# Wide buffers for 4 KB tiles from the MLP on, a third accumulator bank for late up-projections, and the last output block normalized on VectorE

## The chip, the cores and the metric

The kernel runs on one core of one Trainium2 chip. Its metric is the device time of one execution in microseconds (us). The core's engines are TensorE (PE, with its weight loads shown apart as PEld), VectorE (DVE), ScalarE (ACT), GpSimd (POOL) and SyncE (SP), which here only issues transfers. Each engine works through its own list of instructions in order. On-chip data lies in SBUF (128 partitions); matmul results lie in PSUM banks.

## The reference, cut to what matters

One layer of a two-branch encoder, run over two batches with the same weights: a prompt of 512 rows and a sample of 1024 rows, 1024 wide.

```python
def _trunk(x, ...):
    h = _rmsnorm(x, norm_attn_g[l])
    z = h @ w_in[l]
    ...
    a_out = _window_attn(q, k, v, bias, band, attn_sink[l])
    c = ca * jax.nn.sigmoid(cb)
    c = _dwconv(c, conv_dw_w[l], conv_dw_b[l])                # 31 taps
    c = jax.nn.silu(_layernorm(c, conv_ln_g[l], conv_ln_b[l]))
    x = x + jnp.concatenate([a_out, c], axis=-1) @ w_out[l]
    h = _rmsnorm(x, norm_ffn_g[l])
    u = _dwconv(h @ w_up[l], ffn_dw_w[l], ffn_dw_b[l])        # 3 taps
    x = x + (jax.nn.silu(u[..., :D_FF]) * u[..., D_FF:]) @ w_down[l]
    return _rmsnorm(x, norm_final_g)
```

All is float32, D_FF is 2816, and the outputs are the two normalized batches.

## The kernel before

**Precision.** A float32 product is made of three matmuls on operands split into a high and a low part (high·high, high·low, low·high). `split` does this for a weight: the raw tile comes by a transfer (`chunk_raw`, L224, 128x8x128 float32 = 512 KB), ACT makes the high part (L230, CAST), POOL subtracts it to get the low part (L231, 128x1024; for some tiles DVE does). `proj` issues the three matmuls for each of eight slices of the inner dimension (L347, L348, L350).

**Stages.** Up to about 250 us: the input projections (results in banks named b), with the convolution taps of the conv branch on DVE (L402) and ACT (L394). From about 250 to 620 us the prompt's MLP runs: 22 steps `ffn_step(k)`, each with two up-projections, a gate half and a value half (`up_half`), whose accumulators are banks u0 and u1. Of each up-projection's bank ACT makes the scaled copy with the middle tap (L973), and DVE adds the two neighbours (L969), after which the bank is free. `gate` then multiplies the halves (DVE L997, L999; POOL or DVE L1000) and stores the product in DRAM as gt0 to gt10 (L1001). Between the MLP's matmuls the attention, conv norm and out-projection of the sample are woven in as side work (`sample`): attention scores (L674, L681), the concatenated rows stored and reloaded (catd, L757, L780; ACT L766 casts them on arrival), conv norms of blocks of 128 rows (cvd loaded at L787, transposed at L804, statistics on DVE, the power of -0.5 on POOL in `rstd_of`, L214 and L215, normalized by DVE at L810, transposed back at L816), and the out-projection (L840 to L842). From about 620 to 670 us PE works off what is left of this side work.

**Pair sums.** `pair_sums(p)` loads gt of one pair (L1016, 512 KB) into a buffer of kind c, makes four sums and differences on POOL in a second buffer of kind c (L1023, L1025, L1027, L1029, each 128x256) and stores them as gb (L1030). For the pairs 0 to 6 and 10 this comes late in the prompt's stretch; pairs 7 to 9 do it at once, without the load.

**Sample's MLP and the end.** From about 680 us on the sample's MLP runs, in a fixed order on PE that is written out by hand (up-projections L1229 to L1231, down-projections L1579 to L1581), until 1483 us. At the end, for each block of 128 rows, DVE adds the last product to the running sum (L1089), and `finish` normalizes: the mean square of the right half (ACT L1637, the left half's was made before in `left_first`), the mean of both (POOL L1640), the power (POOL L1641), then ACT scales the left half (L1646) while DVE scales the right half (L1650), and SP issues both stores (L1651, 256 KB each).

**What sets the order.** `Slots` hands out named SBUF buffers: 15 of kind q (4096 bytes for each partition), 4 of kind c (4224 bytes), 61 of kind h (2048) and smaller ones. `Slots.tile` takes the smallest kind that fits and of it the one at the head of the free list. So a 4 KB tile takes a q buffer while one is free, and a c buffer only if none is. The c buffers hold the padded rows of the conv branch up to about 325 us, then the pair sums. Which instruction stands where in each engine's list is fixed when the program is built, by when its operands and its buffer come free in the build's own reckoning; SP's list too: a load that gets a buffer which has long been free moves ahead in it. From the sample's MLP on PE's order is by hand. `banks` hands out PSUM banks in the same way; `use["up"]` is the list of kinds that an up-projection may take.

Tile names as the order lists give them are buffer, number of the tile in the buffer pool, and a number of the program: `c2_620_4101` is tile 620 in buffer c2. `qsd`, `ksd`, `bbd`, `catd`, `cvd`, `x1d`, `gt`, `gb` are arrays in DRAM.

Of the kernel before, what the change touches and what calls it, by code (L numbers as in the profile page):

```python
# [15 lines left out]
P = 128  # L16
# [57 lines left out]
class Slots:  # L74
# [3 lines left out]


    def __init__(self, pool, classes, halved=None, keep=0):  # L80
        self.pool, self.free, self.n, self.clock, self.since, self.old = pool, [], 0, 0, {}, 0
        self.halved, self.keep, self.halves = halved, keep, {F32: [], F32R: []}
        for kind, (count, size) in classes.items():
            for i in range(count):
                self.free.append((f"{kind}{i}", size))
# [13 lines left out]
    def tile(self, shape, dt=F32, nbytes=4, among=None):  # L99
        self.clock += 1  # L100
        need = nbytes
        for s in shape:
            need *= s
        fits = [s for s in self.free if s[1] >= need and (among is None or s[0][0] in among)]
        least = min((s[1] for s in fits), default=0)
        slot = next((s for s in fits if s[1] == least), None)
        if self.halved and nbytes == 4 and need <= 2048:
            halves = self.halves[dt]
            wholes = [s for s in fits if s[0][0] == self.halved]
            since = self.since.get(slot[0], -OLD) if slot and slot[1] < 4096 else self.clock  # L110
            if halves and (min(h[2] for h in halves) < since or since == self.clock):
                return Half(*self.oldest(halves), shape)
            if (since == self.clock or self.clock - since < self.old) and len(wholes) > self.keep and \
                    self.since.get(wholes[0][0], -OLD) < since:
                self.split_whole(wholes[0], dt)
                return Half(*self.oldest(halves), shape)
        if slot is None:
            raise RuntimeError(f"no slot for {need} bytes")
        self.free.remove(slot)
        self.n += 1  # L120
        return Held(self, slot, (self.pool(slot[0]) if callable(self.pool) else self.pool).tile([P] + list(shape), dt, tag=slot[0], name=f"{slot[0]}_{self.n}", bufs=1))
# [52 lines left out]
def tile_hybrid_encoder(ctx: ExitStack, tc: tile.TileContext, xs, xsT, rel_bias, norm_attn_g, w_in,  # L174
# [39 lines left out]
        nc.gpsimd.tensor_scalar(out, ss, 1.0 / n, EPS, op0=ALU.mult, op1=ALU.add)  # L214
        nc.gpsimd.tensor_tensor(out, out, nhalf[:], op=ALU.pow)  # L215

    def load_x(G, tt):
        x = sb.tile([D])
        nc.sync.dma_start(x[:], G["x"][tt * P:(tt + 1) * P, :])
        return x  # L220

    def chunk_raw(src, col):
# [111 lines left out]
    def drain(queue):  # L334
        while queue:
            advance(queue)
# [604 lines left out]
    load_kv()  # L941
    drain(convs)
    sb.old = 0


    def want_up(k, half):
# [101 lines left out]
    def sample():  # L1048
        sink_columns()
        yield from attention(8, 24)  # L1050
        kt.clear(), vt.clear(), qt.clear(), bias.clear(), score_rows.clear()
        use.update(norm="a")
        pace.update(rate=RN)
        for m in range(KC + WOA):
            if m in (2, 4):
                load_cat(m // 2 + 3)
            if m < KC:
                load_wo(m, 0)
            if m >= WOA:
                split_wo(m - WOA, 0, True)  # L1060
                yield 0.0
        drain(late)
        for m in range(NE):
            yield from conv_norm(4 + m)
        load_conv(4 + NE)
        for kc in range(KC):
            load_wo(kc, 1)
            yield 0.0
# [561 lines left out]
        nc.gpsimd.tensor_scalar(rs[:, 0:1], ss[:, 0:1], 1.0 / D, EPS, op0=ALU.mult, op1=ALU.add)  # L1630
        nc.vector.tensor_tensor(part, part, fins[0][:, L], op=ALU.mult)

    def finish(blk, parts, tail):
        ss, rs, o = early.pop(blk) if tail else (sm(2), sm(2), sb.tile([D]))
        for n in range(1 if tail else 0, 2):
            s = slice(n * NT, (n + 1) * NT)
            nc.scalar.activation(o[:, s], parts[n], AF.Square, accum_out=ss[:, n:n + 1])  # L1637
        if not tail:
            nc.gpsimd.tensor_scalar(rs[:, 0:1], ss[:, 0:1], 1.0 / D, EPS, op0=ALU.mult, op1=ALU.add)
        nc.gpsimd.tensor_scalar(rs[:, 1:2], ss[:, 1:2], 1.0 / D, rs[:, 0:1], op0=ALU.mult, op1=ALU.add)  # L1640
        nc.gpsimd.tensor_tensor(rs[:, 1:2], rs[:, 1:2], nhalf[:], op=ALU.pow)  # L1641
        G, b = (GR[1], blk) if blk >= 0 else (GR[0], blk + 4)
        for n in range(2):
            s = slice(n * NT, (n + 1) * NT)
            if n == 0:
                nc.scalar.activation(o[:, s], parts[n], AF.Identity, scale=rs[:, 1:2])  # L1646
                if not tail:
                    nc.gpsimd.tensor_tensor(o[:, s], o[:, s], fins[0][:, s], op=ALU.mult)
            else:
                nc.vector.scalar_tensor_tensor(o[:, s], parts[n], rs[:, 1:2], fins[0][:, s], op0=ALU.mult, op1=ALU.mult)  # L1650
            nc.sync.dma_start(G["o"][b * P:(b + 1) * P, s], o[:, s])  # L1651
# [132 lines left out]
    for tt in (2, 3):  # L1784
        z = wide()
        for p in range(NPAIR):
            mm_down(z[:, L], 3, p, tt)
        add(cut(o12, tt), z[:, L], cut(o12, tt))
        finish(tt, (cut(o11, tt), cut(o12, tt)), True)
        del z  # L1790
    by_hand.__exit__(None, None, None)

# [53 lines left out]
```

## Time and profile before

| | us |
|---|---|
| three runs | 1492.49, 1493.83, 1494.63 (median 1493.83) |
| profiled execution, by itself | 1492.24 |
| its span (first to last instruction) | 1490.4 |
| PE busy in it | 1471.8 (99%) |
| DVE busy | 1136.2 (76%) |
| ACT busy | 798.0 (54%) |
| POOL busy | 678.0 (45%) |
| bytes moved | 225.6 MB, 151 GB/s over the span |

How to read it: the span is the time from the first to the last instruction that the profile records; 1.84 us of the profiled execution lie around it. A row of the timeline gives start, duration, engine, line of the kernel, operation, `output<-inputs` by name, shapes, a count where equal instructions follow on each other, and in brackets the idle time of the engine ahead of it with the engine and tile that ended it. A row of the waits names the waiting engine, line and bank, what it waited for, and then the sum in us, the number of times, and the longest. In the rows of windows stand the stretch, its length, the busy times of PE, PEld, DVE, ACT and POOL with instruction counts, the granted clock of PE as a share, the mean busy share of the 16 DMA engines and GB/s. `SPq` is the time that SP stands at the issue of transfers. The mean granted clock over the span is 0.998.

### The profile page before, as it was taken

What the parts mean: (1) busy time and instruction counts of PE and PEld (TensorE: products, weight loads), DVE (VectorE), ACT (ScalarE), POOL (GpSimd) and SP (SyncE); (2) the same over time, 40 slices, a digit from 0 to 9 for tenths busy, and PEclk for the clock granted to TensorE, in tenths of its full rate; (3) what the DMA queues carried; (4) which work ended last, traced back from release to release, by engine and by line L of the source; (5) the groups of instructions that cost most, each with busy time, mean ns of one, the idle gap of its engine ahead of it and who ended that gap; (6) DMA issues with size and microseconds to landing.
All of it is one profiled execution on the core that took longest, in us unless ns stands there. A gap on an engine that the chain in (4) does not pass through costs nothing.

```text
span 1490.4 us, 19857 instructions
## 1 busy us (share of the span) xinstructions
PE 1471.8 (99%) x6808; PEld 1218.8 (82%) x6808; DVE 1136.2 (76%) x1616; ACT 798.0 (54%) x1417; POOL 678.0 (45%) x540
## 2 busy tenths in 40 slices
PE   9999999999999999999999999999999999999998
PEld 7788887887888888878888888888887888888886
DVE  5999996888689975666868777777776945569884
ACT  8555656345777776444465544555445633444254
POOL 6962335235665575763326555555544000003345
PEclk9999999999999999999999999999999999999999
DMA  9953246374433347883213333333332672357644
GB/s 316 284 171 92 86 121 184 99 231 128 133 110 121 120 126 224 272 304 131 82 57 106 106 106 106 106 104 99 103 105 80 227 265 85 113 171 233 216 163 170
DMA packets 221905, 225.60 MB, mean 151 GB/s; under 512 B 12347, under 2 KB 161859, under 8 KB 221676
## 3 DMA queue, kind: packets, MB, share of 16 engines
q1 hardware_dynamic: 221804, 224.34, 47.0%
q8 instruction: 53, 0.87, 0.3%
q14 instruction: 48, 0.39, 0.1%
HBM read 165.29 MB, written 60.05 MB: 151 GB/s over the span
## 4 chain that ended last, share of the span: by engine, by line
PE 86%; DMA 5%; DVE 3%; POOL 2%; ACT 1%; issue 1%; SPq 0%; POOLq 0%; ACTq 0%; DVEq 0%
PE w L1229 9%; PE w L1231 9%; PE w L1230 9%; PE w L1580 7%; PE w L1579 7%; PE w L1581 7%; PE u L347 4%; PE u L348 4%; PE u L350 4%; PE b L347 4%; PE b L350 4%; PE b L348 4%; DMA c<-gt 2%; PE u L840 2%; PE u L842 2%; PE u L841 2%
## 5 line engine op out<-in xcount | busy, mean ns | idle before, releaser
L231 POOL TENSOR_TENSOR q<-q,q 128x1024 fp32r<-128x1024 f32 x71 | 172.9, 2439 | 122.8 <-ACT q L230 51.4
L1092 POOL TENSOR_TENSOR q<-q,q 128x512 fp32r<-128x512 f32 x101 | 141.5, 1408 | 151.2 <-ACT q L1215 140.3
L1092 DVE TENSOR_TENSOR h<-h,h 128x512 fp32r<-128x512 f32 (+2 forms) x202 | 157.4, 814 | 65.6 <-ACT h L1096 27.8
L1581 PE MATMUL w<-h,h 128*128 128x512 f32 x462 | 179.7, 389 | 0.0
L1579 PE MATMUL w<-h,h 128*128 128x512 f32 x458 | 178.2, 389 | 0.0
L1580 PE MATMUL w<-h,h 128*128 128x512 f32 x458 | 178.2, 389 | 0.0
L1229 PE MATMUL w<-h,q 128*128 128x512 f32 x448 | 174.9, 390 | 1.3 <-ACT w L1312 1.1
L1231 PE MATMUL w<-h,q 128*128 128x512 f32 x448 | 174.3, 389 | 0.0
L1230 PE MATMUL w<-h,q 128*128 128x512 f32 x426 | 165.8, 389 | 0.0
L402 DVE SCALAR_TENSOR_TENSOR c<-c,cvw,c 128x512 f32<-128x512 f32 x209 | 157.0, 751 | 3.1
L347 PE MATMUL u<-h,q 128*128 128x512 f32 x368 | 146.9, 399 | 1.9 <-DVE h L969 1.9
L348 PE MATMUL u<-h,q 128*128 128x512 f32 x368 | 144.0, 391 | 0.0
L350 PE MATMUL u<-h,q 128*128 128x512 f32 x360 | 141.2, 392 | 0.0
L1089 POOL TENSOR_TENSOR q<-q,q 128x1024 f32<-128x1024 f32 x12 | 33.1, 2772 | 229.4 <-DVE q L1089 212.9
L1096 ACT CAST h<-h 128x512 fp32r<-128x512 f32 x120 | 72.1, 622 | 97.1 <-DVE h L1092 40.5
L347 PE MATMUL b<-h,q 128*128 128x512 f32 x264 | 104.9, 397 | 0.9 <-DVE q L437 0.9
L230 ACT CAST q<-q 128x1024 fp32r<-128x1024 f32 (+1 forms) x73 | 75.7, 1041 | 54.5 <-POOL q L231 20.6
L348 PE MATMUL b<-h,q 128*128 128x512 f32 x264 | 103.7, 393 | 0.0
L350 PE MATMUL b<-h,q 128*128 128x512 f32 x264 | 103.5, 393 | 0.0
L1581 PEld LDWEIGHTS w<-h,h 128*128 128x128 f32 x462 | 86.7, 188 | 18.0
L1579 PEld LDWEIGHTS w<-h,h 128*128 128x128 f32 x458 | 86.0, 188 | 18.0
L1580 PEld LDWEIGHTS w<-h,h 128*128 128x128 f32 x458 | 86.0, 188 | 17.7
(443 smaller groups left out, 3625.1 us busy)
## 6 DMA issues: line engine op xcount, KB each, us to landing
q<-in_w_up SPq DMA_DIRECT2D x88, 512.0 KB, 4.3
ga<-q SPq DMA_DIRECT2D x64, 256.0 KB, 2.0
h<-ga SPq DMA_DIRECT2D x57, 256.0 KB, 3.4
q<-in_w_in SPq DMA_DIRECT2D x28, 512.0 KB, 5.1
h<-in_w_down SPq DMA_DIRECT2D x52, 256.0 KB, 4.0
q<-in_x_sample SPq DMA_DIRECT2D x15, 512.0 KB, 6.2
h<-qsd SPq DMA_DIRECT2D x23, 256.0 KB, 3.3
x1d<-q SPq DMA_DIRECT2D x11, 512.0 KB, 5.2
```

What stands on the lines that cost most here:

```text
L231: ins = (nc.vector if dve else nc.gpsimd).tensor_tensor(lo[:], raw[:], hi[:].bitcast(F32), op=ALU.subtract)
L347: nc.tensor.matmul(out, whi[:, kc, :], hi[:], start=(kc == 0), stop=False)
L348: nc.tensor.matmul(out, whi[:, kc, :], lo[:], start=False, stop=False)
L350: nc.tensor.matmul(out, wlo[:, kc, :], hi[:], start=False, stop=(kc == KC - 1))
L402: nc.vector.scalar_tensor_tensor(acc[:], src(t), w(t), acc[:], op0=ALU.mult, op1=ALU.add)
L1092: (eng or nc.vector).tensor_tensor(out, a, b, op=ALU.subtract)
L1229: nc.tensor.matmul(out, whi[:, s], hi[:], start=(start and c == 0), stop=False, **go)
L1230: nc.tensor.matmul(out, whi[:, s], lo[:], start=False, stop=False, **go)
L1231: nc.tensor.matmul(out, wlo[:, s], hi[:], start=False, stop=(stop and c == 3), **go)
L1579: nc.tensor.matmul(out, sh[:, c], th[:], start=(p == 0), stop=False)
L1580: nc.tensor.matmul(out, sh[:, c], tl[:], start=False, stop=False)
L1581: nc.tensor.matmul(out, sl[:, c], th[:], start=False, stop=(p == NPAIR - 1))
```

## The change

It has three parts. First, `Slots` gets a field `wide`, 0 until the prompt's MLP begins and 1 from there on: a tile that would take a 4 KB buffer may then take a c buffer instead, if more than one of those is free and the c buffer has been free for longer. Second, in `sample`, after `drain(late)` (about 590 us), `use.update(up="uc")` lets up-projections take the bank c0 besides u0 and u1. Third, `finish` gets `pieces`, true for the sample's fourth block alone, the last to be finished: the mean square of its right half, added to the left half's, comes from one VectorE instruction, so that POOL has only the power to do; DVE makes the right half in two quarters of 128x256, each stored at once by SP, and ACT issues the store of the left half. (`load_x` also gets an argument `halves`, which no caller sets.)

```diff
@@ -78,7 +78,7 @@
 
 
     def __init__(self, pool, classes, halved=None, keep=0):
-        self.pool, self.free, self.n, self.clock, self.since, self.old = pool, [], 0, 0, {}, 0
+        self.pool, self.free, self.n, self.clock, self.since, self.old, self.wide = pool, [], 0, 0, {}, 0, 0
         self.halved, self.keep, self.halves = halved, keep, {F32: [], F32R: []}
         for kind, (count, size) in classes.items():
             for i in range(count):
@@ -104,6 +104,10 @@
         fits = [s for s in self.free if s[1] >= need and (among is None or s[0][0] in among)]
         least = min((s[1] for s in fits), default=0)
         slot = next((s for s in fits if s[1] == least), None)
+        if slot and least == 4096 and among is None and self.wide:
+            spare = [s for s in fits if s[1] > least]
+            if len(spare) > self.wide:
+                slot = min([slot] + spare, key=lambda s: self.since.get(s[0], -OLD))
         if self.halved and nbytes == 4 and need <= 2048:
             halves = self.halves[dt]
             wholes = [s for s in fits if s[0][0] == self.halved]
@@ -214,9 +218,16 @@
         nc.gpsimd.tensor_scalar(out, ss, 1.0 / n, EPS, op0=ALU.mult, op1=ALU.add)
         nc.gpsimd.tensor_tensor(out, out, nhalf[:], op=ALU.pow)
 
-    def load_x(G, tt):
+    def power(out):
+        nc.gpsimd.tensor_tensor(out, out, nhalf[:], op=ALU.pow)
+
+    def mean_square(x, junk, so_far, out):
+        nc.vector.tensor_tensor_reduce(junk, x, x, 1.0 / D, so_far, ALU.mult, ALU.add, out)
+
+    def load_x(G, tt, halves=False):
         x = sb.tile([D])
-        nc.sync.dma_start(x[:], G["x"][tt * P:(tt + 1) * P, :])
+        for s in (slice(0, NT), slice(NT, D)) if halves else (slice(0, D),):
+            nc.sync.dma_start(x[:, s], G["x"][tt * P:(tt + 1) * P, s])
         return x
 
     def chunk_raw(src, col):
@@ -941,6 +952,7 @@
     load_kv()
     drain(convs)
     sb.old = 0
+    sb.wide = 1
 
 
     def want_up(k, half):
@@ -1060,6 +1072,7 @@
                 split_wo(m - WOA, 0, True)
                 yield 0.0
         drain(late)
+        use.update(up="uc")
         for m in range(NE):
             yield from conv_norm(4 + m)
         load_conv(4 + NE)
@@ -1630,15 +1643,18 @@
         nc.gpsimd.tensor_scalar(rs[:, 0:1], ss[:, 0:1], 1.0 / D, EPS, op0=ALU.mult, op1=ALU.add)
         nc.vector.tensor_tensor(part, part, fins[0][:, L], op=ALU.mult)
 
-    def finish(blk, parts, tail):
+    def finish(blk, parts, tail, pieces=False):
         ss, rs, o = early.pop(blk) if tail else (sm(2), sm(2), sb.tile([D]))
-        for n in range(1 if tail else 0, 2):
-            s = slice(n * NT, (n + 1) * NT)
-            nc.scalar.activation(o[:, s], parts[n], AF.Square, accum_out=ss[:, n:n + 1])
-        if not tail:
-            nc.gpsimd.tensor_scalar(rs[:, 0:1], ss[:, 0:1], 1.0 / D, EPS, op0=ALU.mult, op1=ALU.add)
-        nc.gpsimd.tensor_scalar(rs[:, 1:2], ss[:, 1:2], 1.0 / D, rs[:, 0:1], op0=ALU.mult, op1=ALU.add)
-        nc.gpsimd.tensor_tensor(rs[:, 1:2], rs[:, 1:2], nhalf[:], op=ALU.pow)
+        if pieces:
+            mean_square(parts[1], o[:, R], rs[:, 0:1], rs[:, 1:2])
+        else:
+            for n in range(1 if tail else 0, 2):
+                s = slice(n * NT, (n + 1) * NT)
+                nc.scalar.activation(o[:, s], parts[n], AF.Square, accum_out=ss[:, n:n + 1])
+            if not tail:
+                nc.gpsimd.tensor_scalar(rs[:, 0:1], ss[:, 0:1], 1.0 / D, EPS, op0=ALU.mult, op1=ALU.add)
+            nc.gpsimd.tensor_scalar(rs[:, 1:2], ss[:, 1:2], 1.0 / D, rs[:, 0:1], op0=ALU.mult, op1=ALU.add)
+        power(rs[:, 1:2])
         G, b = (GR[1], blk) if blk >= 0 else (GR[0], blk + 4)
         for n in range(2):
             s = slice(n * NT, (n + 1) * NT)
@@ -1646,6 +1662,15 @@
                 nc.scalar.activation(o[:, s], parts[n], AF.Identity, scale=rs[:, 1:2])
                 if not tail:
                     nc.gpsimd.tensor_tensor(o[:, s], o[:, s], fins[0][:, s], op=ALU.mult)
+                if pieces:
+                    nc.scalar.dma_start(G["o"][b * P:(b + 1) * P, s], o[:, s])
+                    continue
+            elif pieces:
+                for h in (slice(NT, NT + HT), slice(NT + HT, W2)):
+                    nc.vector.scalar_tensor_tensor(o[:, h], parts[n][:, h.start - NT:h.stop - NT], rs[:, 1:2],
+                                                   fins[0][:, h], op0=ALU.mult, op1=ALU.mult)
+                    nc.sync.dma_start(G["o"][b * P:(b + 1) * P, h], o[:, h])
+                continue
             else:
                 nc.vector.scalar_tensor_tensor(o[:, s], parts[n], rs[:, 1:2], fins[0][:, s], op0=ALU.mult, op1=ALU.mult)
             nc.sync.dma_start(G["o"][b * P:(b + 1) * P, s], o[:, s])
@@ -1786,7 +1811,7 @@
         for p in range(NPAIR):
             mm_down(z[:, L], 3, p, tt)
         add(cut(o12, tt), z[:, L], cut(o12, tt))
-        finish(tt, (cut(o11, tt), cut(o12, tt)), True)
+        finish(tt, (cut(o11, tt), cut(o12, tt)), True, tt == 3)
         del z
     by_hand.__exit__(None, None, None)
 
```

The lists of instructions hold the same work but for the last block: PE has as many instructions as before, DVE three more, POOL one fewer. Of 2166 tiles 396 get another buffer, the first of them the raw tile 594 of w_up. PE's list differs only by rows that change places locally, from about 255 us on. The engines' lists change as follows at the places below. Line numbers of the changed kernel are larger by 11 to 13 from `chunk_raw` up to `finish` (L224 is L235, L347 is L358, L1016 is L1028, L1029 is L1041); L214 and L215 are L218 and L219.

SP's list at about 328 us: loads of queries and keys for the sample's attention (qsd, ksd, into q and h buffers) and three raw tiles of w_up. Before:

```order
L638 DMA h38_549_3651<-qsd1_164 128x512
L623 DMA h17_517_3434<-bbd_400 128x384
L638 DMA h51_578_3841<-qsd1_164 128x512
L877 DMA q9_501_3377<-ksd_167 64x1024 x2
L638 DMA h59_556_3698<-qsd1_164 128x512
L224 DMA q13_525_3510<-in_w_up 128x8x128
L224 DMA q4_510_3420<-in_w_up 128x8x128
L224 DMA q7_519_3438<-in_w_up 128x8x128
```

and now:

```order
L649 DMA h38_549_3651<-qsd1_164 128x512
L634 DMA h17_517_3434<-bbd_400 128x384
L235 DMA c2_620_4101<-in_w_up 128x8x128
L649 DMA h51_578_3841<-qsd1_164 128x512
L888 DMA q9_501_3377<-ksd_167 64x1024 x2
L649 DMA h59_556_3698<-qsd1_164 128x512
L235 DMA q13_525_3510<-in_w_up 128x8x128
L235 DMA q4_510_3420<-in_w_up 128x8x128
L235 DMA q7_519_3438<-in_w_up 128x8x128
```

The raw tile 620 of w_up, before taken into buffer q14 18 rows further on, stands in c2 ahead of three loads of the attention and of the three raw tiles 525, 510 and 519.

PE's list at about 617 us, where the up-projections 346, 348 and 350 are the prompt's last, a1_352 is a transpose of a conv norm, and c0_358 is an out-projection. Before:

```order
L350 MATMUL u0_346_6305<-h10_494_3319,q7_952_6221 128x512
L804 MATMUL a1_352_6473<-ident_91,h56_1007_6461 128x128 x4
L840 MATMUL c0_358_6612<-h22_963_6259,h1_994_6387 128x512
L841 MATMUL c0_358_6612<-h25_964_6260,h1_994_6387 128x512
L842 MATMUL c0_358_6612<-h22_963_6259,h18_995_6388 128x512
L840 MATMUL c0_358_6612<-h24_966_6271,h1_994_6387 128x512
L347 MATMUL u1_348_6370<-h5_478_3229,q6_974_6301 128x512
```

and now:

```order
L361 MATMUL u0_346_6305<-h10_494_3319,c3_952_6221 128x512
L361 MATMUL c0_350_6425<-h5_478_3229,q4_987_6353 128x512
L358 MATMUL c0_350_6425<-h12_480_3238,q8_986_6352 128x512
L359 MATMUL c0_350_6425<-h20_481_3239,q8_986_6352 128x512
L361 MATMUL c0_350_6425<-h12_480_3238,q4_987_6353 128x512
L358 MATMUL c0_350_6425<-h9_484_3259,q8_986_6352 128x512
L359 MATMUL c0_350_6425<-h8_485_3260,q8_986_6352 128x512
L358 MATMUL u1_348_6370<-h5_478_3229,q14_974_6301 128x512
```

The up-projection 350, before in u0 behind the other two, now has its own bank c0 and six of its matmuls stand between the end of 346 and the start of 348; the out-projection c0_358 comes later.

SP's list where the load of pair 1's gt stands (tile 1066): before behind the store gb8, at about 606 us, into buffer c2:

```order
L1030 DMA gb8_3409<-c2_937_6113 128x1024
L1016 DMA c2_1066_6760<-gt1_3391 128x1024
L224 DMA q10_954_6230<-in_w_up 128x8x128
L787 DMA h36_1020_6541<-cvd1_170 128x4x128
L780 DMA h34_1021_6543<-catd_168 128x512
```

and now behind the load of the x_sample block 1124, which in before's list was issued at about 633 us, into buffer c0, which held the sums stored as gb9:

```order
L1042 DMA gb9_3410<-c0_989_6362 128x1024
L876 DMA h37_1025_6568<-in_w_out 64x512 x2
L878 DMA h31_1030_6598<-in_w_out 128x512
L878 DMA h26_1031_6600<-in_w_out 128x512
L230 DMA q8_1124_7075<-in_x_sample 128x1024
L1028 DMA c0_1066_6760<-gt1_3391 128x1024
L1042 DMA gb2_3403<-c3_1102_6957 128x1024
```

That load has moved down by more than 20 rows of SP's list. POOL's list at about 650 us, with the last sums of pair 3 (tile 1120), the sums of pair 6 (tile 1169) and the power for a conv norm (s10_1060). Before:

```order
L1025 TENSOR_TENSOR c3_1120_7066<-c2_1117_7045 128x256
L1027 TENSOR_TENSOR c3_1120_7066<-c3_1120_7066,c2_1117_7045 128x256
L1029 TENSOR_TENSOR c3_1120_7066<-c2_1117_7045,c3_1120_7066 128x256
L1000 TENSOR_TENSOR h45_1029_6593<-h45_1029_6593,h57_1028_6588 128x512
L1023 TENSOR_TENSOR c0_1169_7346<-c1_1168_7344 128x256
L1025 TENSOR_TENSOR c0_1169_7346<-c1_1168_7344 128x256
L1027 TENSOR_TENSOR c0_1169_7346<-c0_1169_7346,c1_1168_7344 128x256
L214 TENSOR_SCALAR s10_1060_6692<-s8_1059_6691 128x1
L1029 TENSOR_TENSOR c0_1169_7346<-c1_1168_7344,c0_1169_7346 128x256
L215 TENSOR_TENSOR s10_1060_6692<-s10_1060_6692,nhalf_92 128x1
```

and now:

```order
L1035 TENSOR_TENSOR c2_1120_7066<-c0_1117_7045 128x256
L1037 TENSOR_TENSOR c2_1120_7066<-c0_1117_7045 128x256
L1039 TENSOR_TENSOR c2_1120_7066<-c2_1120_7066,c0_1117_7045 128x256
L1041 TENSOR_TENSOR c2_1120_7066<-c0_1117_7045,c2_1120_7066 128x256
L218 TENSOR_SCALAR s10_1060_6692<-s8_1059_6691 128x1
L219 TENSOR_TENSOR s10_1060_6692<-s10_1060_6692,nhalf_92 128x1
L1035 TENSOR_TENSOR c3_1169_7346<-c1_1168_7344 128x256
L1037 TENSOR_TENSOR c3_1169_7346<-c1_1168_7344 128x256
L1039 TENSOR_TENSOR c3_1169_7346<-c3_1169_7346,c1_1168_7344 128x256
L1041 TENSOR_TENSOR c3_1169_7346<-c1_1168_7344,c3_1169_7346 128x256
```

Both rows of the power now stand ahead of the sums of pair 6, and behind those of pair 3; before, they stood among those of pair 6. Elsewhere: the raw tile 594 is loaded about at 250 us, ahead of loads of w_out; between the store of gb7 and the load of catd rows into tile 957 (567 to 578 us) SP issued four loads of 512 KB, the tiles 913, 1064 (gt0), 985 and 917, and issues five now, 917, 1053, 990, 1036 and 933, of which 1036 and 1053 are x_sample blocks that came between 614 and 620 us; and DVE's L810 for the conv norm at about 677 us (with POOL's power for it) stands one place ahead of a scaling of rows (L1110).

## The prediction

> **What bounds the kernel now.** The page comes first: PE is busy for nearly the whole span.
>
> ```profile
> span 1490.4 us, 19857 instructions
> PE 1471.8 (99%) x6808; PEld 1218.8 (82%) x6808; DVE 1136.2 (76%) x1616; ACT 798.0 (54%) x1417; POOL 678.0 (45%) x540
> ```
>
> All that PE doesn't do is 18.6 us, and start and end hold most of it. The change touches the stretch from 240 us on, so I read PE's waits from there to PE's end, and the windows of that stretch.
>
> ```profile
> PE u L347 <- DVE h L969: 1.9, 3, 0.7
> PE a L816 <- DVE h L810: 1.0, 2, 0.5
> PE u L840 <- ACT h L230: 0.4, 1, 0.4
> ...
> 240.00:730.00 490.00, 486.06 (x2312) 403.22 (x2311) 375.29 (x633) 287.30 (x536) 270.62 (x210) 1.00 0.52 164
> 326.00:342.00 16.00, 15.48 (x82) 12.79 (x81) 10.07 (x14) 8.66 (x12) 12.34 (x9) 1.00 1.06 335
> 567.00:570.50 3.50, 3.50 (x19) 2.96 (x18) 2.00 (x6) 2.47 (x6) 1.69 (x1) 1.00 0.55 196
> 570.50:584.50 14.00, 14.00 (x72) 11.70 (x71) 6.33 (x14) 8.07 (x17) 8.77 (x7) 1.00 1.00 283
> 612.00:660.00 48.00, 46.63 (x215) 37.47 (x213) 29.92 (x43) 16.33 (x31) 35.62 (x41) 1.00 0.94 316
> ```
>
> The reader is to see two things. Buffers and banks can take from PE only those few waits, 3.3 us by these three rows. And the DMA engines, half idle on the whole (0.52), are full at three places (1.06, 1.00, 0.94): there a load put ahead delays those behind it. The granted clock is 1.00 throughout, so it is no term.
>
> **The sum is made against the profiled execution**, 1492.24 us, of which 1.84 lie outside the span; the median of the runs, 1493.83, is 1.59 above it. I add the terms to the median. A difference under 0.2% (3.0 us: from 1490.8 to 1496.8) can't be told from none.
>
> **Part A, the last block.** Nothing covers it: PE is done.
>
> ```profile
> 1483.47 0.69 DVE L1089 TENSOR_TENSOR q<-w,q 128x512 f32<-128x512 f32 x1 [1.82 <-PE w L1581]
> 1485.37 0.55 POOL L1641 TENSOR_TENSOR s<-s,nhalf 128x1 f32<-128x1 f32 x1
> 1485.95 0.75 DVE L1650 SCALAR_TENSOR_TENSOR q<-q,s,c 128x512 f32<-128x512 f32 x1 [1.79 <-POOL s L1641]
> 1486.70 0.81 SPq L1651 DMA_DIRECT2D out_sample<-q  x2
> ...
> L681 DVE CUSTOM_DVE_ANT_0 q<-a,h,nsink 128x384 f32<-128x384 f32 x31 | 18.7, 615 | 4.5 <-PE a L674 4.3
> L681 DVE CUSTOM_DVE_ANT_0 q<-a,h,nsink 128x256 f32<-128x256 f32 x13 | 6.0, 481 | 2.9 <-PE a L674 2.9
> L681 DVE DVE_READ_ACCUMULATOR2_ANT s<- 128x1 f32 x96 | 8.1, 84 | 0.0
> L1092 DVE TENSOR_TENSOR h<-h,h 128x256 fp32r<-128x256 f32 x7 | 2.9, 420 | 3.4 <-ACT h L1563 1.8 <-PE w L1580 1.6
> ```
>
> The trace has no such reduction. Its nearest rows are the attention's reducing instruction: 481 ns at 256 columns, 615 at 384, so 134 for 128 more and an estimated 0.75 us at 512, and 0.08 for reading the accumulator. The add ends at 1484.16; 0.83 of reduction and an estimated 0.13 to reach POOL (POOL's own handover to DVE took 0.03, from 1485.92 to 1485.95) put the power's start at 1485.13, against 1485.37 in the row: 0.24 earlier. Then come the scalings. Before, both halves ended near 1486.70 and SP needed 0.81 for both stores, to 1487.51. Now the first quarter (0.42, by the 128x256 row) ends near 1486.13, the second near 1486.55, SP issues them by 1486.95 (0.40 each), and ACT issues the left half beside it. So the last issue ends 0.56 earlier. I take −0.5. The upper bound comes from the landing:
>
> ```profile
> out_sample<-q SPq DMA_DIRECT2D x8, 256.0 KB, 2.2
> x1d<-q SPq DMA_DIRECT2D x11, 512.0 KB, 5.2
> ```
>
> A store that ACT issues isn't in the trace. The nearest row is the same store issued by SP, 2.2; the far one is 5.2, 3.0 more: ACT's issue ends 0.66 before 1487.51, so the end would be 2.3 later (the bound below is −0.6). I go by 2.2, since bytes and target are the same. [...]
>
> **Part B, the load of tile 594 at 250 us.**
>
> ```profile
> 257.68 0.50 PE L840 MATMUL u<-h,h 128*128 128x512 f32 x1 [0.39 <-ACT h L230]
> ```
>
> A w_out load is what this wait hangs on, through ACT's cast. 512 KB more ahead of it cost 0.52 MB at 335 GB/s, 1.56 us. But PE's list now has nine more matmuls ahead of this one, and at 490 us for 2312 they cover 1.9 us. I take 0. Bounds: −0.4 (the wait goes and the load finds idle DMA) and +1.5 (no cover).
>
> **Part C, the load of tile 620 at 328 us.** Here the DMA engines are full.
>
> ```profile
> 332.20 4.64 SPq L224 DMA_DIRECT2D q<-in_w_up  x3
> 339.91 1.05 ACT L230 CAST q<-q 128x1024 fp32r<-128x1024 f32 x1 [4.89 <-DMA q<-in_w_up]
> 345.39 0.47 PE L347 MATMUL u<-h,q 128*128 128x512 f32 x1 [0.61 <-DVE h L969]
> 352.20 0.47 PE L347 MATMUL u<-h,q 128*128 128x512 f32 x1 [0.62 <-DVE h L969]
> ```
>
> ACT's list stands still for 4.89 us for such a load, L973 for the up-projection is queued behind its casts, DVE's L969 behind that, and PE waits for L969. All three are in order, so 1.56 us more of DMA reach PE whole: +1.56. The second wait (352.20) goes, because on DVE one conv tap (L402) moves from between the two L969 to ahead of the first, where DVE idles anyway: −0.62. Together +0.94. Bounds: −1.23 (the load costs nothing and both waits go) and +1.56. [...]
>
> **Part D, five loads for four between 567 and 578 us.**
>
> ```profile
> 578.30 0.58 SPq L780 DMA_DIRECT2D h<-catd  x1
> 583.88 0.62 ACT L766 CAST h<-h 128x512 fp32r<-128x512 f32 x1 [4.47 <-DMA h<-catd]
> 587.68 0.75 DVE L969 SCALAR_TENSOR_TENSOR h<-u,fw,h 128x511 f32<-128x511 f32 x1
> 589.90 0.48 PE L347 MATMUL u<-h,q 128*128 128x512 f32 x1
> ```
>
> ACT waits for the catd rows, and the next L973 and L969 stand behind. 0.52 MB more at 283 GB/s are 1.85 us; the first loads now fall into 567 to 570.5 at share 0.55, where 0.45 × 3.5 = 1.6 us are free: 0.25 late. L969 ends at 588.43 and PE needs it at 589.90, a margin of 1.47. So 0; without the idle stretch it is 0.4.
>
> **Part E, the third bank.**
>
> ```profile
> 617.29 0.48 PE L347 MATMUL u<-h,q 128*128 128x512 f32 x1 [0.69 <-DVE h L969]
> ```
>
> PE waits here for u1 to come free. Six matmuls of 350 now stand ahead, 1.3 us of work that needs no such bank; the waiting is 0.69 and goes. −0.69, or 0 if the split of tile 987 for it is late.
>
> **Part F, POOL between 628 and 680 us.**
>
> ```profile
> 631.75 0.74 POOL L1023 TENSOR_TENSOR c<-c 128x256 f32<-128x256 f32 x1 [0.49 <-DMA gb<-c]
> 634.42 1.29 POOL L1029 TENSOR_TENSOR c<-c,c 128x256 f32<-128x256 f32 x1
> 654.13 0.55 POOL L215 TENSOR_TENSOR s<-s,nhalf 128x1 f32<-128x1 f32 x1
> 654.72 0.81 DVE L810 TENSOR_SCALAR h<-a,s,s 128x512 f32<-128x512 f32 x1 [2.83 <-POOL s L215]
> 655.67 0.63 PE L816 MATMUL a<-ident,h 128*128 128x128 f32 x4 [0.54 <-DVE h L810]
> ...
> 632.73 0.60 SPq L219 DMA_DIRECT2D q<-in_x_sample  x1
> ...
> c<-gt SPq DMA_DIRECT2D x8, 512.0 KB, 6.9
> ```
>
> The power now runs ahead of pair 6's sums: by itself that ends the wait of 0.54 at 655.67. But pair 1's gt is loaded only behind an x_sample load, at 633.3 by this row. Landing after 6.9 (the median) at 640.2, its four sums, 3.96 us from 631.75 to 635.71, end at 644.2 instead; gt3 takes the same buffer (0.4, then 6.9, then 3.96) and ends at 655.4, and the power behind it at about 656.3 instead of 654.68: +1.6. On the other hand two x_sample blocks have left the stretch (share 0.94). With landings one us shorter the power ends at 654.3. I take 0 for this wait and −0.4 for the second one of the row L816, 1.0 − 0.54, where the power of a conv norm moves ahead of others. F is −0.4, bounds −0.95 and +1.6.
>
> **The rest.** In the steady steps the w_up loads come earlier and PE doesn't wait; 0. In the sample's MLP the changed buffers stand ahead of no wait on them: 0.
>
> **Sum:** −0.5 + 0 + 0.94 + 0 − 0.69 − 0.4 = −0.65, or 1491.6 for the profiled execution and **1493.2** by the median.
>
> **The rivals.**
>
> *Faster: an early load is free.* The DMA share is 0.52, so those behind catch up. A −0.5, B −0.4, C −1.23, E −0.69, F −0.95: −3.8, 1490.0. For it: over the whole stretch half the DMA is free. Against it: ACT's 4.89 us in a window at 1.06. Chance 0.20. [...]
>
> *Slower: the pair sums hold POOL.* The wide buffers that now go to split weights are missing for gt1, and POOL in order stands before the sums of pair 1 and of pair 3, with the powers for the conv norms behind. In before one gt took longer than the median:
>
> ```profile
> 649.24 3.01 SPq L1016 DMA_DIRECT2D c<-gt  x1
> 658.12 0.74 POOL L1023 TENSOR_TENSOR c<-c 128x256 f32<-128x256 f32 x1 [3.44 <-DMA c<-gt]
> ```
>
> That is 8.9 us from issue to use. Two links of 8.9 end the power at 633.3 + 8.9 + 3.96 + 0.4 + 8.9 + 3.96 + 0.9 = 660.3, 5.6 later; with A, C and E the sum is +5.35, 1499.2. It decides once the power ends later than 657.9 (F above +3.2). For it: the median alone gives 656.3. Against: less is in flight. 0.12.
>
> *ACT's store lands late:* A is +2.3 instead of −0.5, 1496.0. 0.08.
>
> *It does nothing:* buffers and banks aren't what PE waits for and the tail's reduction is no shorter: 1493.8. 0.05.
>
> **How the numbers follow.** The forecast keeps 0.55. Its own bounds reach from 1490.6 (all lower ends) to about 1497 (ends above combined as roots of squares: 2.8, 1.5, 0.6, 0.4, 0.7 and 2.0 give 3.8). The range takes in the faster rival and ACT's late store and leaves out the slower one: 1489.8 to 1497.0. Faster is the first rival, 0.20; slower the second, 0.12; the same is the rest, 0.68.
>
> **What would show it.** Right: no PE wait on L981 (which was L969) near 352 and 617, one of about 2.2 near 345; the last issue ended 0.5 sooner after the last matmul; the power for the transpose near 655 between 653.5 and 655.5 when moved to before's clock. Wrong: pair 3's sums ending past 657, an ACT store landing over 3 us after its issue, or waits at places that had none, above all for a split at the prompt's last up-projections.

## The result: slower by 0.8%, and the profile after

The changed kernel took 1504.18 us (median of six runs, 1501.48 to 1506.29), the kernel before 1492.59 beside it (six runs, 1491.95 to 1494.63). The ratio is 1.0078, 95% interval 1.0068 to 1.0089. The profiled execution of the changed kernel has a span of 1503.0 us against 1490.4. The page and the waits of PE from 230 us on, in the same form as before:

```profile
span 1503.0 us, 19863 instructions
...
PE u L358 <- DVE h L981: 3.5, 1, 3.5
PE u L358 <- DVE s L818: 3.1, 1, 3.1
PE w L1242 <- ACT w L1325: 2.2, 1, 2.2
PE t L1165 <- DVE h L1105: 1.3, 1, 1.3
PE u L361 <- POOL c L242: 1.0, 1, 1.0
PE w L1242 <- ACT h L1334: 0.9, 1, 0.9
```

Few waits, but long ones: 13.0 us in all (1.0 of it in small rows left out here), against 5.4 before. That is 7.6 of the 12.6 us by which the span grew. The rest shows only in the windows behind the three longest waits. The first number behind the last pair of brackets is the granted clock:

```profile
346.00:350.00 4.00, 2.97 (x7) 2.42 (x8) 3.90 (x9) 2.24 (x3) 4.00 (x3) 0.51 0.21 63
350.00:354.00 4.00, 4.00 (x13) 3.11 (x13) 3.67 (x7) 1.65 (x3) 2.92 (x2) 0.63 0.01 2
354.00:358.00 4.00, 4.00 (x21) 3.37 (x20) 2.66 (x10) 2.31 (x7) 0.45 (x1) 1.00 0.22 49
...
626.00:630.00 4.00, 4.00 (x12) 3.12 (x11) 3.85 (x6) 0.74 (x2) 3.70 (x6) 0.57 0.82 295
630.00:634.00 4.00, 4.00 (x21) 3.31 (x20) 0.72 (x2) 1.16 (x3) 2.20 (x3) 1.00 0.86 293
...
812.00:818.00 6.00, 4.38 (x12) 3.48 (x13) 5.93 (x6) 2.11 (x4) 3.03 (x2) 0.72 0.44 171
```

PE counts as busy in them and does little: 13 matmuls in the 4 us from 350 on and 12 from 626 on, where at 0.227 us for each some 18 of 512 columns fit. Added up matmul by matmul, the extra time behind the three waits is 2.85, 1.75 and 1.7 us, 6.3 us in all. Waits and lower clock, 13.9, less 0.4 gained at the end and 0.8 at the start give 12.7 of the 12.6 us. (PE stood at 257.5 instead of 258.7 us by its 1225th matmul; 0.4 of these 1.2 is a wait that is counted already. This start isn't the change's: 0.5 of it is there at 108 us, before the change acts, and the rest also shows in two later runs that have before's order up to 1200 us.)

**The place at 345 us.** SP, ACT and PE in the changed kernel:

```profile
328.16 0.44 SPq L235 DMA_DIRECT2D c<-in_w_up  x1
341.58 1.05 ACT L241 CAST q<-q 128x1024 fp32r<-128x1024 f32 x1 [7.79 <-DMA q<-in_w_up]
347.03 0.77 PE L358 MATMUL u<-h,q 128*128 128x512 f32 x1 [3.49 <-DVE h L981]
```

The first row is the load of tile 620 that moved ahead. ACT's cast comes at 341.58 instead of 339.91, 1.67 us later, and PE waits until 347.03 instead of 345.39. One pair of profiles doesn't show how much of this is the load: further down, the same wait differs by 1.4 us between executions with one order.

**The place at 615 us.** POOL, DVE, SP and PE, and the landing of the gb stores between 596 and 640 us:

```profile
606.69 0.33 SPq L1042 DMA_DIRECT2D gb<-c  x1
...
DMA to landing us min/median/max: 2.7/5.3/6.5
...
613.33 2.37 POOL L242 TENSOR_TENSOR c<-q,q 128x1024 fp32r<-128x1024 f32 x1 [6.66 <-DVE h L981]
615.75 0.50 PE L361 MATMUL u<-h,c 128*128 128x512 f32 x1 [1.04 <-POOL c L242]
616.90 5.20 POOL L242 TENSOR_TENSOR q<-q,q 128x1024 fp32r<-128x1024 f32 x2
616.98 5.67 DVE L242 TENSOR_TENSOR h<-h,h 128x512 fp32r<-128x512 f32 x2 [3.09 <-POOL h L1012]
625.50 0.47 PE L358 MATMUL u<-h,q 128*128 128x512 f32 x1 [3.10 <-DVE s L818]
```

POOL stands still for 6.66 us ahead of the subtraction that writes the low part 952 into c3. The row names DVE, but what this instruction waits for by the program are the raw tile and the store of gb8 out of c3. The store, issued at 606.69 and the slowest of the four (6.5), lands at 613.2; POOL's wait for the semaphore of that landing ends at 613.24, and POOL starts at 613.33. Then PE waits 1.04 for the subtraction. POOL then makes its two other subtractions back to back, and two of DVE's, which take 0.68 each alone, last 5.67 together beside them. The taps that free u1 stand behind them on DVE: 3.10 us.

**The place at 811 us**, in the sample's MLP:

```profile
803.34 2.88 POOL L1105 TENSOR_TENSOR q<-q,q 128x512 fp32r<-128x512 f32 x2 [2.57 <-ACT q L1228]
804.99 0.38 SPq L1192 DMA_DIRECT2D q<-in_w_up  x1
808.90 0.69 DVE L1105 TENSOR_TENSOR h<-q 128x512 f32<-128x512 f32 x1 [5.09 <-DMA q<-in_w_up]
813.00 0.57 ACT L1325 COPY w<-w 128x512 f32<-128x512 f32 x1 [5.32 <-DVE q L1372]
813.62 0.71 PE L1242 MATMUL w<-h,q 128*128 128x512 f32 x1 [2.24 <-ACT w L1325]
```

A split of raw tile 6 runs late on ACT and POOL, to 804.96; the load of raw tile 12 takes the same buffer and is issued at 804.99; DVE waits 5.09 for it with the taps L1371 and L1372 queued behind, ACT for these, PE for ACT. Before, the longest wait of PE in this MLP was

```profile
PE w L1229 <- ACT w L1312: 1.1, 1, 1.1
```

**The end**, where the last block is finished:

```profile
1497.19 0.75 DVE L225 CUSTOM_DVE_ANT_0 q<-q,s 128x512 f32<-128x512 f32 x1
1498.03 0.55 POOL L222 TENSOR_TENSOR s<-s,nhalf 128x1 f32<-128x1 f32 x1 [6.60 <-DVE s L225]
1499.13 0.81 SPq L1672 DMA_DIRECT2D out_sample<-q  x2
1499.36 0.37 ACTq L1666 DMA_DIRECT2D out_sample<-q  x1
...
out_sample<-q ACTq DMA_DIRECT2D x1, 256.0 KB, 2.2
```

From PE's end (1496.42) to the span's end it is 6.57 us, against 7.00 before.

### The profile page after: what moved, and what is told of

Same layout as the page of the kernel before. It is cut to its first block, busy times and chain, and to the rows that moved or that the text cites. A ratio compares the mean times of both kernels' runs of the same rounds, so it can differ in the third digit from the quotient of the medians.

```text
span 1503.0 us, 19863 instructions
## 1 busy us (share of the span) xinstructions
PE 1478.0 (98%) x6808; PEld 1223.3 (81%) x6808; DVE 1130.6 (75%) x1619; ACT 794.5 (53%) x1415; POOL 679.4 (45%) x539
## 4 chain that ended last, share of the span: by engine, by line
PE 88%; DVE 4%; issue 2%; DMA 2%; POOL 2%; ACT 1%; SPq 0%; POOLq 0%; DVEq 0%; ACTq 0%
PE w L1242 8%; PE w L1243 8%; PE w L1244 8%; PE w L1594 7%; PE w L1592 7%; PE w L1593 7%; PE u L358 5%; PE u L359 5%; PE u L361 5%; PE b L358 4%; PE b L361 4%; PE b L359 4%; PE u L853 2%; PE u L851 2%; PE u L852 2%
## 5 line engine op out<-in xcount | busy, mean ns | idle before, releaser
L242 POOL TENSOR_TENSOR q<-q,q 128x1024 fp32r<-128x1024 f32 x51 | 124.0, 2438 | 98.6 <-ACT q L241 65.3
L1105 POOL TENSOR_TENSOR q<-q,q 128x512 fp32r<-128x512 f32 x72 | 100.4, 1397 | 123.1 <-ACT q L1228 120.4
L361 PE MATMUL u<-h,q 128*128 128x512 f32 x336 | 132.7, 395 | 0.0
L358 PE MATMUL u<-h,q 128*128 128x512 f32 x312 | 125.9, 404 | 6.6 <-DVE h L981 3.5
L1242 PE MATMUL w<-h,q 128*128 128x512 f32 x308 | 121.2, 394 | 3.3 <-ACT w L1325 2.2
L359 PE MATMUL u<-h,q 128*128 128x512 f32 x312 | 123.9, 397 | 0.0
L1244 PE MATMUL w<-h,q 128*128 128x512 f32 x308 | 120.4, 391 | 0.0
L1243 PE MATMUL w<-h,q 128*128 128x512 f32 x299 | 117.1, 392 | 0.0
L1105 POOL TENSOR_TENSOR c<-q,c 128x512 fp32r<-128x512 f32 x56 | 79.6, 1422 | 73.0 <-ACT c L1228 72.0
L358 PE MATMUL b<-h,q 128*128 128x512 f32 x264 | 104.8, 397 | 0.9 <-DVE q L448 0.9
L1102 POOL TENSOR_TENSOR q<-c,q 128x1024 f32<-128x1024 f32 x2 | 4.8, 2392 | 210.6 <-DVE c L1102 210.6
```

Source lines behind the costliest of these rows:

```text
L242: ins = (nc.vector if dve else nc.gpsimd).tensor_tensor(lo[:], raw[:], hi[:].bitcast(F32), op=ALU.subtract)
L358: nc.tensor.matmul(out, whi[:, kc, :], hi[:], start=(kc == 0), stop=False)
L359: nc.tensor.matmul(out, whi[:, kc, :], lo[:], start=False, stop=False)
L361: nc.tensor.matmul(out, wlo[:, kc, :], hi[:], start=False, stop=(kc == KC - 1))
L1105: (eng or nc.vector).tensor_tensor(out, a, b, op=ALU.subtract)
L1242: nc.tensor.matmul(out, whi[:, s], hi[:], start=(start and c == 0), stop=False, **go)
```

## The experiments

**Theory A:** the wide buffers cost all of it, in two ways: they put transfers and instructions behind work that they didn't wait for before, and PE's waits that come of it are followed by a lower clock. **Rival B:** the third bank and the finish do. **Rival C:** the loads' order is of no matter.

### Without the wide buffers

```diff
-    sb.wide = 1
```

> The change without its first part: wide stays 0, the third bank and the new finish are kept. Theory A (the wide buffers cost all of it, by waits and by the clock that falls behind the long ones): 1491.5 to 1493, no lower clock after 340, 620 and 810 us. Rival B (the third bank lets PE run into the wait of 3.1 us at 622 us of the changed kernel, and the tail does the rest): about 1497 to 1498, with the wait of PE on u1 still over 2 us there. The tail (PE's end to the span's end) 6.6 us by both, as in the changed kernel, against 7.0.

1492.07 us, ratio 0.9999 (0.9990 to 1.0008). PE's longest wait from 230 us on is 1.17 and the clock isn't lowered behind any:

```profile
PE u L358 <- DVE h L980: 2.6, 3, 1.2
PE a L827 <- DVE h L821: 0.9, 2, 0.6
...
618.78 0.47 PE L358 MATMUL u<-h,q 128*128 128x512 f32 x1 [1.17 <-DVE h L980]
```

So all of the slowdown needs the wide buffers; B falls. The third bank by itself doesn't take the wait at 617 us away: it is 1.17 here, 0.69 before.

### The wide buffers alone

```diff
-        use.update(up="uc")
...
-        finish(tt, (cut(o11, tt), cut(o12, tt)), True, tt == 3)
+        finish(tt, (cut(o11, tt), cut(o12, tt)), True)
```

> The first part alone: wide buffers, no third bank, the old finish. A: 1503 to 1506, with the waits of PE near 343, 614 to 625 and 811 us. B: about 1497 to 1499, the wait at 622 us gone or under 1 us.

1506.47 us, ratio 1.0094 (1.0080 to 1.0108): 0.5 us above A's range and far from B's, with waits of 4.3, 1.1, 3.1 and 2.3 us at the same places. The wait on u1 is there without the third bank.

### The low part 952 not in a wide buffer

```diff
-        if slot and least == 4096 and among is None and self.wide:
+        if slot and least == 4096 and among is None and self.wide and self.n + 1 not in (952,):
```

> The whole change, but the low part 952 of one weight may not take a wide buffer. A, with the chain store gb8 to buffer c3 to POOL's subtraction to DVE to PE at 614 to 626 us as one of three places: POOL's idle time of 6.7 us there goes, PE's waits of 1.0 and 3.1 us go, the clock stays at 1.00 there, and the kernel is 3.5 to 5.5 us faster than the changed one, about 1499. B: the wait on u1 stays, since six matmuls of the third bank's projection cover only 1.3 us; no more than 1 us faster, about 1503.

1503.11 us, ratio 1.0070 (1.0055 to 1.0086): by time at most about 1 us better than the changed kernel (the two intervals overlap), as B expected and not the 3.5 to 5.5 of A; by the trace the chain is gone as A expected. No wait on u1 is left and the clock at 626 is 1.00. But two others took its place: 1.6 us at 619, for the cast of the weight of projection 350, whose load was issued at 611.7, and this one:

```profile
658.69 0.55 POOL L219 TENSOR_TENSOR s<-s,nhalf 128x1 f32<-128x1 f32 x1
660.23 0.63 PE L827 MATMUL a<-ident,h 128*128 128x128 f32 x4 [2.27 <-DVE h L821]
...
626.00:630.00 4.00, 4.00 (x21) 3.37 (x20) 2.98 (x5) 2.50 (x6) 2.74 (x4) 1.00 0.84 268
660.00:664.00 4.00, 3.52 (x12) 2.65 (x13) 2.76 (x6) 2.65 (x6) 0.35 (x2) 0.70 0.83 277
```

This is the prediction's slower rival: the conv norm's power on POOL behind pair sums that are late. In the changed kernel PE was itself too late by then to see it.

### The raw tile 620 not in a wide buffer

The same line with `(620,)`.

> The whole change, but the raw tile 620 may not take a wide buffer, so that its load goes back behind the three loads that ACT waits for at about 340 us. A: PE's wait of 3.5 us at 343 us falls to about 1.5 (the 0.6 of before and what PE has gained ahead of it), the clock stays at 1.00 there, the kernel is 3 to 4 us faster than the changed one, about 1500.5. Rival C (the DMA is full there whatever its order, and ACT's list waits as long): the wait stays over 2.5 us and the time at 1504.

1502.92 us, ratio 1.0075 (1.0061 to 1.0088). The wait at 343 us is 2.07 us in the profiled execution, with no lower clock behind it, and its span is 1500.4, 2.6 shorter. The runs don't confirm that: by time this is inconclusive. 2.07 instead of 3.49 speaks against C, but one profile doesn't settle it, as the next run shows.

### One load alone

The kernel before with one tile forced into c2:

```diff
+        if slot and least == 4096 and among is None and self.wide and self.n + 1 == 620:
+            spare = [s for s in fits if s[0] in ("c2", "c3")]
+            if spare:
+                slot = min(spare)
```

> The kernel before, with one thing of the change: the raw tile 620 is loaded into buffer c2, ahead of the three loads that ACT waits for at about 340 us; no third bank, the old finish. By the sum of the prediction the load of 512 KB costs 1.56 us in the DMA queues and the wait at 345 us becomes 2.2 us instead of 0.6. Clock theory (a wait of PE of about 2.05 us or more is followed by some 3 us of matmuls at nearly half the rate): this lies on the edge, +1.6 us without and +3.3 with the fall, 1493.8 to 1495.5. Rival (an early load is free): no change, 1492.2, wait 0.6.

1494.37 us against 1491.39, ratio 1.0018 (1.0007 to 1.0029), about 2.7 us:

```profile
345.07 0.47 PE L358 MATMUL u<-h,q 128*128 128x512 f32 x1 [1.94 <-DVE h L981]
345.00:349.00 4.00, 3.93 (x11) 3.16 (x12) 3.87 (x9) 2.77 (x5) 4.00 (x3) 0.61 0.32 96
```

The wait of 0.6 is one of 1.94, and 11 matmuls stand in the 4 us behind it. But the load isn't all that differs: SP's and PE's lists change at further places too. And the profiled execution is the fastest of its ten (1490.57): by its matmuls PE loses 2.1 us at 345 and has them back by 700 us. That the 2.7 us of the runs arise at this place isn't shown.

The wait also varies with nothing changed. Here it is in the two runs with set waits (below), which have before's order up to 1200 us; the second is followed by a lower clock:

```profile
345.25 0.47 PE L347 MATMUL u<-h,q 128*128 128x512 f32 x1 [1.60 <-DVE h L969]
346.98 0.47 PE L347 MATMUL u<-h,q 128*128 128x512 f32 x1 [2.02 <-DVE h L969]
```

So all twelve profiles have to be taken together. In the six with a load of w_up moved ahead at this place the wait is 1.94 to 4.30 us, 3.15 on the mean; in the six without, 0.61 to 2.38, 1.58 on the mean. By these an early load costs about 1.6 us here and isn't free.

### Wide only up to the sample's MLP

```diff
     h2.pop((0, 0))
+    sb.wide = 0
```

> The whole change, but wide goes back to 0 when the sample's MLP begins. A with the fourth place put down to choices made in that MLP: PE's wait of 2.2 us at 811 us and the lower clock after it go, about 1500. A with that place put down to the buffers that the prompt's part leaves behind: the wait stays, 1504.

1497.34 us, ratio 1.0039 (1.0028 to 1.0050), faster than either expectation. PE's waits of 1.3, 2.2 and 0.9 us after 690 us are gone; the longest that is left there is

```profile
PE w L1243 <- ACT w L1326: 0.8, 1, 0.8
```

About half of the slowdown came of buffers handed out in the sample's MLP, in which the prediction had put 0.

### The three places mended

All of it: neither 620 nor 952 wide, and wide off at the sample's MLP.

> The whole change, but the tiles 620 and 952 may not take a wide buffer and wide goes back to 0 at the sample's MLP. A: the waits over 2.05 us near 343 and 622 us go and with them the lower clock there; what is left is the power at about 657 us (2.3 us of wait when 952 alone is narrow) and, if the fourth place stays, 811 us. 1496 to 1499. If all long waits went: about 1492.5, the same as before.

1495.27 us, ratio 1.0023 (1.0013 to 1.0034), 0.7 below A's range. Waits of 2.4 us at 345, 2.3 at 619 and 2.7 at 662 are left, with a lower clock behind the first two. A had the long waits at the first two places go, and missed: with both tiles narrow PE still waits there.

### Wide in the middle of the prompt only

```diff
-    sb.wide = 1
...
     for k in range(NJ):
+        sb.wide = int(4 <= k < 18)
...
+    sb.wide = 0
```

> The whole change, but wide is 1 only during the prompt's steps 4 to 17 of 22. The load of tile 624 now takes buffer c2, free since 325 us, and stands in SP's list where 620 stood, though its step comes 25 us later. Theory (what counts is since when the buffer is free, not when the rule is switched on): PE waits 2.4 to 3.5 us near 345, mostly with a lower clock after it, no other wait over 1.5 us from there on, 1494.5 to 1496.5. Rival (switched on after the place, the rule does no harm and the early loads of the steady steps even help): 0.6 us of wait at 345, 1490 to 1492.

1495.28 us against 1490.55, ratio 1.0028 (1.0015 to 1.0041). PE waits 3.3 us at 346, with 1.7 us lost behind it, and 1.9 at 640, which wasn't expected. The load of tile 624 stands where 620 stood. So it isn't the moment at which the rule is switched on that counts, but since when the buffer is free; and no gain from the early loads of the steady steps shows.

### Waits of a set length

The kernel before, with a chain of VectorE operations that add zero to an operand of the down-projections, one in each of six products:

```diff
...
+            if w == 0:
+                th = hl[i, NPAIR - 2][1][0]
+                for n in STALL[i]:
+                    nc.vector.scalar_tensor_tensor(th[:, 0:n], z[:, W2 - n:W2], 0.0, th[:, 0:n].bitcast(F32), op0=ALU.mult, op1=ALU.add)
...
```

> The kernel before, with six chains of VectorE put ahead of an operand of the down-projections, so that PE waits once in each of six products, for about 1.2, 1.9, 2.3, 2.6, 3.3 and 4.7 us (products 2, 5, 6, 7, 4 and 1); nothing is left out. Clock theory: the waits up to about 1.9 us cost just themselves and the clock stays at 1.00; those from 2.3 us on are followed by matmuls 0.43 us apart instead of 0.23 for 3 to 5 us, 1.5 to 2.9 us more each, in all about 16 us of waits and 7 to 10 us of lower clock. Rival (the lower clock of the changed kernel has nothing to do with its waits): the clock stays at 1.00 after all six, or falls where there was none.

> As the run with six long waits, but with chains of 128, 256, 384, 640, 896 and 1536 columns (products 2, 5, 6, 7, 4 and 1); nothing is left out. By the waits seen so far (below 1.8 us none of eight was followed by a lower clock, from 1.8 to 2.6 some were, from 2.7 on nearly all): waits of about 1.2 to 3.1 us, none of those below 1.8 followed by a lower clock, one or two of those between 1.8 and 2.6. Rival (a sharp threshold): all above one length, none below it.

Two waits of the first of these runs with the window behind each:

```profile
1315.19 0.50 PE L1579 MATMUL w<-h,h 128*128 128x512 f32 x1 [2.53 <-DVE h L1684]
1410.72 0.80 PE L1579 MATMUL w<-h,h 128*128 128x512 f32 x1 [3.21 <-DVE h L1684]
1315.00:1319.00 4.00, 3.81 (x17) 3.17 (x18) 0.82 (x2) 2.40 (x3) 0.00 (x0) 1.00 0.00 0
1410.50:1414.50 4.00, 3.78 (x9) 3.00 (x10) 1.30 (x2) 0.62 (x1) 2.38 (x1) 0.50 0.00 0
```

Two of the second, with windows of 3.41 us each, the one in which most of the wait lies and the next:

```profile
1398.30 0.50 PE L1579 MATMUL w<-h,h 128*128 128x512 f32 x1 [2.01 <-DVE h L1684]
1447.22 0.50 PE L1579 MATMUL w<-h,h 128*128 128x512 f32 x1 [2.12 <-DVE h L1684]
1395.40:1398.81 3.41, 1.40 (x6) 0.85 (x6) 2.74 (x5) 0.62 (x1) 0.00 (x0) 1.00 0.15 56
1398.81:1402.22 3.41, 3.41 (x9) 2.68 (x9) 0.57 (x1) 0.62 (x1) 2.37 (x1) 0.50 0.06 17
1443.19:1446.60 3.41, 1.91 (x9) 1.25 (x7) 3.21 (x6) 1.72 (x4) 0.00 (x0) 1.00 0.93 281
1446.60:1450.01 3.41, 2.79 (x12) 2.29 (x13) 2.92 (x3) 0.17 (x1) 0.00 (x0) 1.00 0.51 191
```

Waits made on purpose lower the clock: after 1.83, 3.21, 3.43 and 6.60 us in the first run (1.7, 2.9, 2.8 and 3.0 us lost), after 2.23 and 2.01 in the second (1.7 each). After 1.97 and 2.53 in the first, and 0.65, 0.97, 1.46 and 2.12 in the second, it stays at 1.00. So the cause is the wait, but not its length alone. The lengths didn't come out as meant: 1.83 to 6.60 us in the first run for 1.2 to 4.7, 0.65 to 2.23 in the second for 1.2 to 3.1.

What the two kinds differ in is shown by the traces' records of the granted clock. Up to PE's last matmul all twelve traces together have 24 stretches of lowered clock. Each begins a whole number of times 3.413 us after the record in which the clock first goes up, and lasts one, two or three times 3.413 us. In the changed kernel the clock first goes up at 4.78 us, and the lowered stretches begin at 346.12 (100 times 3.413 us later, for two), 626.01 (182, for one) and 813.74 (237, for one). Of the 3.413 us ahead of each PE stood idle for 2.57, 2.90 and 2.24, of any other such window that ends before PE does for 1.27 at most; in the kernel before it is 1.04 at most, and the clock isn't lowered. The four windows of the second run above are cut at these marks. The wait of 2.01 us lies in one of them (PE is busy for 1.40 of 3.41), and the next is granted 0.50. The wait of 2.12 is cut into 1.50 and 0.62, and the clock stays; so is the wait of 2.53, into 1.62 and 0.91. Over all 88 waits of 0.6 us and more from 50 us on, the clock fell behind 24 of the 25 that left PE idle for 1.83 us or more within one such window (not behind one of 1.86), and behind none of the 63 with 1.77 or less. So in these profiles the two kinds part at about 1.8 us, but for that one, when the idle time is counted by these windows and not by the whole wait.

## Why the prediction was wrong

**Slower by 0.8% where no change was forecast.** Two steps failed, and with them the term E. Added up by place, PE lost 4.8 us at 345, 5.2 at 615 to 626 and 6.2 in the sample's MLP, and got back 2.1 between 650 and 700; the 6.3 us of lower clock are part of the first three.

*"The granted clock is 1.00 throughout, so it is no term."* No wait of before from 230 us on was longer than 1.1 us, and in the twelve profiles from 50 us on none below 1.8 us was followed by a lower clock. The change lengthened waits, and I priced each by its length alone. The extra 6.3 us stand behind three of them, of 3.49, 3.10 and 2.24 us.

*"In the sample's MLP the changed buffers stand ahead of no wait on them: 0."* I read the waits of before there and not the order of what was to come. With wide off from there on, 1.0078 becomes 1.0039. There the rule changed which buffer each split gets; a buffer that is free in the build's reckoning has a last reader that in the run comes late, and the next load of that buffer with it.

The other parts, by their own terms:

- **A**, −0.5: 0.43 by the two tails. Right, and steady: 6.55 to 6.57 us in all seven profiles with the new finish, 7.00 in all five without. The estimated 0.13 to reach POOL was 0.08 (the accumulator read ends at 1497.95, the power starts at 1498.03). ACT's store landed after 2.2 us, as the row of SP's had it; the rival of a late landing is out.
- **B**, 0 (bounds −0.4 and 1.5): the wait of 0.4 on the w_out split is gone, and PE gains 0.7 with it. But it is missing in the two runs with set waits too, with the same gain and before's order; so this isn't shown to be the change's.
- **C**, +0.94: mechanism and size right on the mean of the twelve profiles (1.6 us more wait, 1.56 put). In this pair the cast came 1.67 later, the wait at 352 is gone (so it is in one of the runs with before's order), and PE came 1.2 earlier, so the wait is 3.49 and the net about 1.0. That the pair agrees so well is in part luck, since 0.61 is the shortest wait of the six profiles without the load. Missing are the 2.85 us of lower clock behind it.
- **D**, 0: no wait at 590 in the changed kernel. Right.
- **E**, −0.69: wrong. In its place stand 1.04 and 3.10, from one store that had not left its buffer. Alone the third bank leaves 1.17. I had named a late split as the bound, with 0 as its price.
- **F** and its rival: the mechanism that I gave 0.12, sums and powers held on POOL by buffers that the weights took, was the right family. It came first 40 us earlier and the other way round, a weight's subtraction waiting for a sum's store, and at the expected place (2.27 us at 660) once that was mended.
- **The faster rival**, an early load is free: the twelve profiles speak against it at this place (3.15 us of wait on the mean with the load, 1.58 without), where the window row shows the DMA engines full (1.06).
- **The bounds**: two sums don't come out. The lower ends of the parts add up to −3.87, so to 1490.0 and not 1490.6, and the upper ones combine to 3.9 and not 3.8. Neither brings 1504 near.

What stays open: how much of the time at 345 us a single early load costs, since no run has that load and else before's lists; what else makes PE wait at 345 and 619 us with 620 and 952 narrow; and which single tile in the sample's MLP starts the chain at 811 us. That raw tile 6 was read late is shown, and that it goes with the rule; the tile whose buffer was the first to be late wasn't isolated. A load in a wide buffer that is kept from moving up in SP's list wasn't run.

## What to carry to other kernels

Price a wait of TensorE not by its length alone: here 24 of the 25 that left it idle for 1.83 us or more within one window of 3.413 us, as cut above, cost 1.7 to 3 us on top, so a wait that grows from 0.6 to 2.0 us can cost 3 instead of 1.4. Look at one place in more than one profile: with nothing changed a wait here was 0.6, 1.6 and 2.0 us. When a pool's rule for handing out buffers changes, every later tile may get another buffer: look in the new order at what each buffer held last and when that is read or stored out, above all for results that leave by a slow store (here 6.5 us from issue to landing). A load into a buffer that has long been free moves up to wherever SP's list lets it, so ask whose transfer is behind it in a stretch where the DMA engines are full (share 1.06 here).

## What the runs showed of the hardware

**The lower clock behind a wait.** Over all profiled executions here, from 50 us on: none of 35 waits of 0.9 to 1.8 us was followed by it, 12 of 18 between 1.8 and 2.8 were, and 12 of 12 of 2.9 and more. Matmuls of 512 columns then start 0.43 us apart instead of 0.227, mostly for one window of 3.413 us (1.7 us lost). Where the wait reaches 0.87 us or more into the first lowered window, a second follows (2.8 to 3.0 lost); where it reaches at most 0.37 into it, none does. Nearly equal lengths go either way (2.01 and 2.12 in one run). Counted by the idle time within one window of 3.413 us, cut from the record in which the clock first goes up, the clock fell behind 24 of the 25 waits with 1.83 us and more (the changed kernel's three: 2.24, 2.57 and 2.90) and behind none of the 63 with 1.77 and less. An estimate from these figures, with a limit of 1.85: a wait of 2.0 us is followed by the lower clock at half of its possible places in these windows, one of 3.0 at four of five, one of 3.7 at all.

**VectorE beside GpSimd.** DVE's subtraction of 128x512 with two operands in SBUF took 0.68 us at 611.82 in the changed kernel, where POOL stood idle; two of them beside two of POOL's took 5.67 together at 616.98. So POOL's delay of 6.66 us was passed on to DVE, which waited 3.09 for it, and by DVE to PE as its wait of 3.10.
